# A two-block transformer kernel in which the second block's norms take each reciprocal root as one GpSimd power, and TensorE adds more of the row sums

## The chip, the cores and the metric

The kernel runs on one core of a Trainium2 chip. Its time is the device time of one execution in microseconds; lower is better. All data are 32-bit floats; matrix products are made from values that are split into a high and a low part, three products for each.

## The reference, cut to what matters

256 tokens of 1024 features pass through a first block (an mLSTM mixer and a diff-attention mixer, each with a mixture of experts) and a second block of two layers. Only the norms of the second block matter here. A sub-layer of it computes an output y for one or two streams (stream 0 is x, stream 1 the context ctx; both have 256 tokens), adds it after a norm and a gate, and norms the new stream for the next sub-layer:

```
r1 = rsqrt(mean(y*y) + EPS)               # per token, over D = 1024 features
x  = x + gate * y * r1
r2 = rsqrt(mean(x*x) + EPS)
u  = x * r2 * gain * (1 + scale) + shift  # input of the next sub-layer
```

There are six sub-layers: FFN, mixer (attention), FFN, then FFN, mixer, and a last FFN. The first four have both streams, the last two stream 0 alone.

## The kernel before, in words

The first block ends at about 914 us of the span. The second keeps the streams transposed, features on partitions: x and ctx are 8 tiles of 128 features x 256 tokens (`KT = 8`). Weights come from HBM, are split into `hi` (ScalarE, L371) and `lo` (VectorE, L374) and held in TensorE while the activations `u` or `act` stream through, in threes (L381, L382, L383; below "products").

The class `Output` (L478 to L551) forms the norms of a sub-layer's output. For every output tile d (0 to 7) and stream, `add` (L489) makes one tile `t` of three 128x256 parts, named `ysq` in the trace: y squared (ScalarE, L497), gate*y squared (ScalarE, L498) and gate*y*x (VectorE, L499). d = 0 goes straight to the accumulator `acc`, d = 1 to 5 are added to it by GpSimd and d = 6 by VectorE (L501). For d = 7, `end` lets TensorE sum over features: products of `acc` and of `t` with a matrix of ones, three each (L519), into the PSUM tile `st`. `go_on` delays `end` by one output tile.

`rows(s)` (L532) follows: VectorE copies the sums out of PSUM (`rowsums`, L537), TensorE transposes them (L540, two), VectorE copies 128x6 numbers (`sums`, L541), and `rstd` (L406 to L423) gives r1 in eleven small VectorE instructions on 128x2 (L412 to L422: mean and EPS, a first guess by the bit pattern, two Newton steps). `row` spreads r1 over all partitions by two TensorE transposes (L427, called rb1 here). The sum of squares of the new x is not taken anew: L546 to L549 work it out on 128x2 from the old one, z2 = sum of (gate*y)^2 and xz = sum of gate*y*x. A second `rstd` and a second `row` (rb2) give r2. `update` (L553) then does the stream tile by tile: gate*y*rb1 (L561, VectorE), its addition to x (L562; the first tile VectorE, the others GpSimd), x*gain*rb2 (L569), and the split into `u` (L358, L359 and L361, L362: even tiles by ScalarE and VectorE, odd ones by ScalarE and GpSimd).

The last FFN (`ffn_last`, L728) works by tokens: for each half of 128 tokens it has the sum of squares from ScalarE (L783), the product with the gate (L784), `rstd`, and the final multiply and add (L789) ahead of the store. `start` (L1056) makes the first norm of each stream.

The order on each engine is set when the program is built, by a scheduler that goes by dependences and estimated times; each engine runs its list in order. PSUM has five tiles for products (`mm`), two for transposes (`tp`, where rb1 and rb2 lie too) and one for sums (`st`). Two buffers hold `ysq`.

Names used below: the boundary between two sub-layers with both streams occurs four times, that with stream 0 alone once (into the last FFN, near 2487 us); the boundary after the fourth sub-layer hands over one of the four. "First boundary" is the one near 1277 us.

Of the kernel before, what the change touches and what calls it, by code (L numbers as in the profile page):

```python
# [10 lines left out]
F32 = mybir.dt.float32  # L11
F32R = mybir.dt.float32r
I32 = mybir.dt.int32
AF = mybir.ActivationFunctionType
# [17 lines left out]
READY = 2  # L32

# [201 lines left out]
class Kernel:  # L235
# [188 lines left out]

    def bcast(self, out, col):

        self.nc.tensor.transpose(out, col.to_broadcast([128, 128]), self.ident)  # L427
# [50 lines left out]
    class Output:  # L478
# [10 lines left out]
        def add(self, d, s):  # L489
# [10 lines left out]
            if 0 < d < KT - 1:  # L500
                (nc.vector if d == KT - 2 else nc.gpsimd).tensor_add(self.acc[s], self.acc[s], t)  # L501
# [8 lines left out]
        def end(self, d, s, t):  # L510
            if d == KT - 1:
                self.sums(s, self.acc[s])
                self.sums(s, t)
                self.done(self, s)
# [17 lines left out]
        def rows(self, s):  # L532

            kern, nc, pool = self.kern, self.kern.nc, self.pool
            v = pool.tile([128, 3, 2], F32, tag="sums", name="sums", bufs=2)
            t = pool.tile([128, S], F32, tag="xs", name="rowsums", bufs=kern.xs_bufs)[:96]
            nc.vector.tensor_copy(t, self.st[:96, s * S:s * S + S])  # L537
# [3 lines left out]
            nc.vector.tensor_copy(v, tp.rearrange("p (j q c) -> p q j c", j=2, q=3)[:, :, :, 0])  # L541
            y2, z2, xz = (v[:, q] for q in range(3))
            x2 = pool.tile([128, 2], F32, tag=f"x2_{s}", name="x2", bufs=2)
            r1 = kern.rstd(pool, y2, 2, D, "n")
            rb1 = kern.row(r1)
            nc.vector.tensor_mul(z2, z2, r1)  # L546
            nc.vector.scalar_tensor_tensor(z2, xz, 2.0, z2, op0=ALU.mult, op1=ALU.add)
            nc.vector.tensor_mul(z2, z2, r1)
            nc.vector.tensor_add(x2, self.x2[s], z2)  # L549
            self.x2[s] = x2  # L550
            return rb1, kern.row(kern.rstd(pool, x2, 2, D, "n2"))  # L551
# [176 lines left out]
    def ffn_last(self, ring, pool, u, gate, home, out):  # L728
# [46 lines left out]
        for j in range(2):  # L775
            for f in (NF - 2, NF - 1):
                down(f, j)
            sums = pool.tile([128, 3, 2], F32, tag="sums", name="sums", bufs=2)[:, 0]
# [7 lines left out]
            r = self.rstd(pool, sums, 2, D, "n")[:, :1]  # L786
# [213 lines left out]
    def second_block(self, pool, result):  # L1000
# [3 lines left out]
        for tag, n, b in (*PLACES, ("wraw", 1024, 5)):  # L1004
            pool.tile([128, n], F32R if tag == "act" else F32, tag=tag, name=tag, bufs=b)
        ready, mark = {}, None
# [26 lines left out]

        with self.tc.issue_after(mark.ins):
            self.start(pool, self.u_first, 0)
# [20 lines left out]
    def start(self, pool, u, s):  # L1056

        x2 = self.x2[s] = self.cp.tile([128, 2], F32, name=f"x2_{s}")
        self.nc.vector.tensor_copy(x2, self.x_squares(pool, s))
# [3 lines left out]
        self.pre(pool, u, s, self.row(self.rstd(pool, x2, 2, D, "n")), gs[:, :, 0], mod[:, 0:8, 0])  # L1063
# [801 lines left out]
```

## Time and profile before

| what | value |
|---|---|
| median of 3 runs | 2703.2 us (2702.36 to 2704.69) |
| the profiled execution's own time | 2702.24 us |
| its span in the profile | 2700.4 us |
| TensorE (PE) busy, weight loads (PEld) | 2476.7 us (92%), 1915.4 us (71%) |
| VectorE (DVE) | 1653.1 us (61%) |
| ScalarE (ACT) | 935.7 us (35%) |
| GpSimd (POOL) | 473.4 us (18%) |

Busy times are shares of one execution's span. A timeline row gives start, duration, engine, line, operation, out<-in, count, and in brackets the idle time of that engine just before it with what ended it. The view of waits sums such idle time by instruction and releaser. Line numbers are those of the kernel before; PE, DVE, ACT, POOL and SP are TensorE, VectorE, ScalarE, GpSimd and SyncE.

### The profile page before, as it was taken

How to read it: one execution, taken by the hardware profiler on the slowest of the kernel's cores; microseconds unless marked ns; L12 is line 12 of the kernel's file. 1: busy time of each engine (PE TensorE's matmuls, PEld its weight loads, DVE VectorE, ACT ScalarE, POOL GpSimd, SP SyncE). 2: the span in 40 equal slices, each digit the busy share in tenths (PEclk: the TensorE clock that was granted, in tenths of full speed). 3: DMA queues.
4: the chain of work that ended last, by engine and by line, in shares of the span. 5: the costliest groups of instructions: out<-in, count | busy, mean ns of one | idle time of the engine just before them, and what ended most of it. 6: DMA issues, size and time to landing. Idle time of an engine off the chain costs nothing.

```text
span 2700.4 us, 38571 instructions
## 1 busy us (share of the span) xinstructions
PE 2476.7 (92%) x14614; PEld 1915.4 (71%) x14614; DVE 1653.1 (61%) x3421; ACT 935.7 (35%) x1641; POOL 473.4 (18%) x420
## 2 busy tenths in 40 slices
PE   3988997887999899999899999999899999898998
PEld 3874344566444688888775788888788888786997
DVE  7873125786222368656866777673858665958555
ACT  3541103564011232223327542222432223445543
POOL 2330101544000000002406420000400001534100
PEclk9989998888999899999899999999999999999999
DMA  8789997667999356532340236453247443322453
GB/s 320 276 327 410 420 419 261 232 211 298 381 398 419 141 185 221 168 120 88 135 138 1 79 110 209 154 190 91 74 148 226 155 150 97 118 83 94 160 178 123
DMA packets 123305, 540.62 MB, mean 200 GB/s; under 512 B 14688, under 2 KB 14944, under 8 KB 98272
## 3 DMA queue, kind: packets, MB, share of 16 engines
q1 hardware_dynamic: 123104, 538.00, 55.2%
q8 instruction: 119, 1.95, 0.3%
q14 instruction: 82, 0.67, 0.1%
HBM read 536.90 MB, written 1.05 MB: 199 GB/s over the span
## 4 chain that ended last, share of the span: by engine, by line
PE 56%; DVE 7%; issue 1%; ACT 1%; DMA 1%; POOL 0%; DVEq 0%; SPq 0%; ACTq 0%; POOLq 0%
PE mm L382 16%; PE mm L383 16%; PE mm L381 16%; DVE lo L374 2%; PE tp L383 1%; PE tp L382 1%; PE tp L381 1%; PE mm L868 1%; PE tp L860 1%; PE mm L848 1%; DVE ysq L499 1%; DMA raw<-in_w_ada_dram 1%; ACT hi L371 0%; DVE mx L818 0%; DVE rs_x L412 0%
## 5 line engine op out<-in xcount | busy, mean ns | idle before, releaser
L374 DVE TENSOR_TENSOR lo<-raw,hi 128x512 fp32r<-128x512 f32 (+1 forms) x780 | 574.7, 766 | 381.5 <-ACT hi L371 379.1
L371 ACT ACTIVATE hi<-raw 128x1024 fp32r<-128x1024 f32 (+1 forms) x390 | 404.7, 1044 | 872.3 <-PE mm L382 571.4
L381 PE MATMUL mm<-u,hi 128*128 128x512 f32 (+1 forms) x1608 | 572.8, 360 | 17.5 <-ACT hi L371 9.6
L383 PE MATMUL mm<-u,lo 128*128 128x512 f32 (+1 forms) x1608 | 576.8, 360 | 5.2 <-DVE lo L374 5.2
L382 PE MATMUL mm<-u,hi 128*128 128x512 f32 (+1 forms) x1608 | 578.2, 360 | 2.3 <-POOL u L359 1.3
L381 PEld LDWEIGHTS mm<-u,hi 128*128 128x128 f32 x1608 | 306.9, 193 | 64.5 <-ACT hi L371 11.2
L383 PEld LDWEIGHTS mm<-u,lo 128*128 128x128 f32 x1608 | 310.5, 193 | 49.1 <-DVE lo L374 6.9
L382 PEld LDWEIGHTS mm<-u,hi 128*128 128x128 f32 x1608 | 310.6, 193 | 47.3 <-DVE u L362 2.5
L382 PE MATMUL mm<-act,hi 128*128 128x512 f32 (+1 forms) x612 | 223.0, 364 | 0.1
L381 PE MATMUL mm<-act,hi 128*128 128x512 f32 (+1 forms) x612 | 222.3, 363 | 0.0
L383 PE MATMUL mm<-act,lo 128*128 128x512 f32 (+1 forms) x612 | 222.2, 363 | 0.0
L1691 PE MATMUL mm<-raw,xg 128*32 128x512 f32 x1696 | 199.2, 593 | 1.1 <-DMA raw<-in_moe_gu_dram 1.1
L623 DVE SCALAR_TENSOR_TENSOR junk<-raw,conds 128x1024 f32<-128x1024 f32 x128 | 155.6, 1222 | 66.3 <-DMA raw<-in_w_ada_dram 65.9
L620 POOL TENSOR_TENSOR raw<-raw,cond 128x1024 f32<-128x1024 f32 x48 | 119.9, 2502 | 244.7 <-DMA raw<-in_w_ada_dram 224.8
L501 POOL TENSOR_TENSOR acc<-acc,ysq 128x768 f32<-128x768 f32 x45 | 92.5, 2065 | 394.0 <-DVE ysq L499 348.8
L623 DVE SCALAR_TENSOR_TENSOR raw<-raw,conds 128x1024 f32<-128x1024 f32 x128 | 156.6, 1229 | 2.4
L628 POOL TENSOR_TENSOR mod<-mod,vecs 128x16 f32<-128x16 f32 (+1 forms) x28 | 10.3, 366 | 764.7 <-DVE raw L623 721.4
L1691 PEld LDWEIGHTS mm<-raw,xg 128*32 128x32 f32 x1696 | 63.0, 110 | 112.3 <-issue 107.6
L381 PEld LDWEIGHTS mm<-act,hi 128*128 128x128 f32 x612 | 117.5, 192 | 18.7 <-issue 1.2
L382 PEld LDWEIGHTS mm<-act,hi 128*128 128x128 f32 x612 | 117.7, 192 | 18.2 <-DVE act L351 0.7
L383 PEld LDWEIGHTS mm<-act,lo 128*128 128x128 f32 x612 | 117.5, 192 | 17.2
L1723 DVE TENSOR_TENSOR hy<-hy,tp 128x512 f32<-128x512 f32 x56 | 38.2, 686 | 149.3 <-PE tp L1720 149.1
(458 smaller groups left out, 4102.5 us busy)
## 6 DMA issues: line engine op xcount, KB each, us to landing
raw<-in_moe_gu_dram SPq DMA_DIRECT2D x122, 1024.0 KB, 17.8
raw<-in_w_ada_dram SPq DMA_DIRECT2D x200, 512.0 KB, 4.5
raw<-in_ffn_wi_dram SPq DMA_DIRECT2D x176, 512.0 KB, 4.3
raw<-in_moe_down_dram SPq DMA_DIRECT2D x63, 1024.0 KB, 17.8
raw<-in_ffn_wo_dram SPq DMA_DIRECT2D x48, 448.0 KB, 3.9
raw<-in_w_k_dram SPq DMA_DIRECT2D x32, 512.0 KB, 3.9
raw<-in_ffn_wo_dram SPq DMA_DIRECT2D x24, 512.0 KB, 4.2
raw<-in_ffn_wo_last_dram SPq DMA_DIRECT2D x22, 512.0 KB, 4.1
```

The costliest lines, as they stand in the source:

```text
L371: self.mark = self.nc.scalar.activation(hi[:, :m], raw[:, c:c + m], AF.Copy)
L374: self.nc.vector.tensor_sub(lo[:, i:e], raw[:, c + i:c + e], hi[:, i:e])
L381: nc.tensor.matmul(out, lh, rh, start=start, stop=False, skip_group_check=mixed)
L382: nc.tensor.matmul(out, lh, rl, start=False, stop=False, skip_group_check=mixed)
L383: nc.tensor.matmul(out, ll, rh, start=False, stop=stop, skip_group_check=mixed)
L499: nc.vector.scalar_tensor_tensor(t[:, 2], y, self.gate(d, s), kern.xs(d, s), op0=ALU.mult, op1=ALU.mult)
L501: (nc.vector if d == KT - 2 else nc.gpsimd).tensor_add(self.acc[s], self.acc[s], t)
L620: nc.gpsimd.tensor_mul(out, rows, c)
L623: nc.vector.scalar_tensor_tensor(out, rows, 1.0, c, op0=ALU.mult, op1=ALU.mult, accum_out=mod[:, t, s:s + 1])
L848: nc.tensor.matmul(sc[:, :nk], qk[a][half, 512 + t * 128:640 + t * 128], qk[b][half, :nk], start=(i == 0), stop=(i == 2))
L1691: nc.tensor.matmul(ps[t:t + 32], x[:, t:t + 32], w[i][:, s], start=first, stop=last)
L1723: nc.vector.tensor_add(yv, yv, tp)
```

## The change

- Each `rstd` of `rows`, of `ffn_last` and of the start of stream 0 becomes `rstd2`: one GpSimd instruction that raises a 128x2 tile to the power -0.5 (exponents from a tile `minus_half`). There are 21: two in each of nine `rows`, two in `ffn_last`, one in `start`. The start of stream 1 keeps the VectorE series.
- The sum of squares carried along becomes mean plus EPS, and the new one is put together around r1: the part in z2 uses the reciprocal of m1 (VectorE) instead of r1 squared, so that only the part in xz waits for the power. The numbers are read from PSUM; the copy L541 is gone.
- The copy of the row sums (L537) goes from VectorE to ScalarE.
- `OWN_SUMS = 6, 4`: GpSimd adds d = 1 to 5 (stream 0) or d = 1 to 3 (stream 1); VectorE adds none. The later tiles are summed by TensorE itself, three products of ones for each, each one output tile after its squares. That is one group of three more for stream 0 (five times) and three more for stream 1 (four times): 51 instructions.

```diff
+OWN_SUMS = 6, 4
...
+    def rstd2(self, x, tag):
+
+        y = self.small.tile([128, 2], F32, tag=tag, name="rp_y", bufs=2)
+        self.nc.gpsimd.tensor_tensor(y, x, self.minus_half, op=ALU.pow)
+        return y
...
-            if 0 < d < KT - 1:
-                (nc.vector if d == KT - 2 else nc.gpsimd).tensor_add(self.acc[s], self.acc[s], t)
+            if 0 < d < OWN_SUMS[s]:
+                nc.gpsimd.tensor_add(self.acc[s], self.acc[s], t)
...
         def end(self, d, s, t):
+            if d == OWN_SUMS[s]:
+                self.sums(s, self.acc[s])
+            if d >= OWN_SUMS[s]:
+                self.sums(s, t)
             if d == KT - 1:
-                self.sums(s, self.acc[s])
-                self.sums(s, t)
                 self.done(self, s)
...
-            v = pool.tile([128, 3, 2], F32, tag="sums", name="sums", bufs=2)
             t = pool.tile([128, S], F32, tag="xs", name="rowsums", bufs=kern.xs_bufs)[:96]
-            nc.vector.tensor_copy(t, self.st[:96, s * S:s * S + S])
+            nc.scalar.activation(t, self.st[:96, s * S:s * S + S], AF.Copy)
...
-            nc.vector.tensor_copy(v, tp.rearrange("p (j q c) -> p q j c", j=2, q=3)[:, :, :, 0])
-            y2, z2, xz = (v[:, q] for q in range(3))
-            x2 = pool.tile([128, 2], F32, tag=f"x2_{s}", name="x2", bufs=2)
-            r1 = kern.rstd(pool, y2, 2, D, "n")
+            y2, z2, xz = (tp.rearrange("p (j q c) -> p q j c", j=2, q=3)[:, q, :, 0] for q in range(3))
+            v = kern.small.tile([128, 4, 2], F32, tag="sums", name="sums", bufs=2)
+            m1, inv, w, z = (v[:, i] for i in range(4))
+            nc.vector.tensor_scalar(m1, y2, 1.0 / D, EPS, op0=ALU.mult, op1=ALU.add)
+            r1 = kern.rstd2(m1, "r1")
             rb1 = kern.row(r1)
-            nc.vector.tensor_mul(z2, z2, r1)
-            nc.vector.scalar_tensor_tensor(z2, xz, 2.0, z2, op0=ALU.mult, op1=ALU.add)
-            nc.vector.tensor_mul(z2, z2, r1)
-            nc.vector.tensor_add(x2, self.x2[s], z2)
-            self.x2[s] = x2
-            return rb1, kern.row(kern.rstd(pool, x2, 2, D, "n2"))
+            nc.vector.reciprocal(inv, m1)
+            nc.vector.scalar_tensor_tensor(w, z2, 1.0 / D, inv, op0=ALU.mult, op1=ALU.mult)
+            nc.vector.tensor_add(w, w, self.x2[s])
+            nc.vector.scalar_tensor_tensor(z, xz, 2.0 / D, r1, op0=ALU.mult, op1=ALU.mult)
+            m2 = kern.small.tile([128, 2], F32, tag=f"x2_{s}", name="x2", bufs=2)
+            nc.vector.tensor_add(m2, w, z)
+            self.x2[s] = m2
+            return rb1, kern.row(kern.rstd2(m2, "r2"))
...
-            r = self.rstd(pool, sums, 2, D, "n")[:, :1]
+            nc.vector.tensor_scalar(sums, sums, 1.0 / D, EPS, op0=ALU.mult, op1=ALU.add)
+            r = self.rstd2(sums, "r1")[:, :1]
```

The scheduler puts the instructions in another order with it. In the order of the changed program the lines are higher by 2 to 13: L383 to L385 are the products, L430 the power, L435 `row`, L507 the VectorE square part, L509 the addition to `acc`, L529 the sums, L549 the transposes, L553 to L561 the small steps of `rows`, L573 and L574 the update (L561 and L562 before), L376 `lo`, L727 an addition of the FFN's output.

First place: VectorE at the first boundary, stream 0's `rows`. Before:

```order
L541 COPY sums<-tp 128x6
L412 TENSOR_SCALAR rs_x<-sums 128x2
L413 TENSOR_SCALAR rs_y<-rs_x 128x2
L414 TENSOR_SCALAR rs_z<-rs_x 128x2
L417 TENSOR_SCALAR rs_h<-rs_x 128x2
L415 TENSOR_TENSOR rs_t<-rs_y 128x2
L416 TENSOR_TENSOR rs_t<-rs_t,rs_z 128x2
L418 SCALAR_TENSOR_TENSOR rs_t<-rs_t 128x2
L419 SCALAR_TENSOR_TENSOR rs_y<-rs_t,rs_y 128x2
L715 TENSOR_TENSOR yT<-yT,mm 128x256
L420 TENSOR_TENSOR rs_t<-rs_y 128x2
L499 SCALAR_TENSOR_TENSOR ysq<-yT,gate,ctxT 128x256
```

With the change, on the same engine:

```order
L553 TENSOR_SCALAR sums<-tp 128x2
L376 TENSOR_TENSOR lo<-raw,hi 128x512
L556 RECIPROCAL sums<-sums 128x2
L573 SCALAR_TENSOR_TENSOR xs<-yT,gate,tp 128x256
L557 SCALAR_TENSOR_TENSOR sums<-tp,sums 128x2
L559 SCALAR_TENSOR_TENSOR sums<-tp,rp_y 128x2
L558 TENSOR_TENSOR sums<-sums,x_0_18444 128x2
L574 TENSOR_TENSOR xT<-xT,xs 128x256
L561 TENSOR_TENSOR x_21176<-sums 128x2
L573 SCALAR_TENSOR_TENSOR xs<-yT,gate,tp 128x256
L727 TENSOR_TENSOR yT<-yT,mm 128x256
```

The series and the stream-1 squares between its steps are gone from here; the first update product (L573), which needs rb1, now stands ahead of the steps that lead to the second power, and the squares of stream 1's tiles stand behind stream 0's update.

Second place: TensorE at the same boundary, from the transposes of stream 0's sums to rb2. With the change (before, 26 to 27 products stand between L540, rb1 and the next sums):

```order
L549 MATMUL tp<-consts,rowsums 128x96 x2
L384 MATMUL mm<-act,hi 128x256
L385 MATMUL mm<-act,lo 128x256
L383 MATMUL mm<-act,hi 128x256
L384 MATMUL mm<-act,hi 128x256
L435 MATMUL tp<-consts,rp_y 128x128 x2
...
L529 MATMUL st<-acc,consts 32x256
L435 MATMUL tp<-consts,rp_y 128x128 x2
L529 MATMUL st<-acc,consts 32x256 x2
L529 MATMUL st<-ysq,consts 32x256 x3
```

Four products now stand between the transposes and rb1, and ten and one sum (the rows left out are products) between rb1 and rb2; rb2 stands ahead of stream 1's sums instead of behind them. Behind rb2 follow 42 products and stream 1's sums as far as they are made, and then the 96 products of stream 0's new `u`, with stream 1's last sums, its transposes, rb1 and rb2 among them.

Third place: GpSimd, from the additions of the first boundary on. Before:

```order
L628 TENSOR_TENSOR mod_0_63<-mod_0_63,vecs 128x16 x4
L501 TENSOR_TENSOR acc<-acc,ysq 128x768 x10
L562 TENSOR_TENSOR xT<-xT,xs 128x256 x3
L359 TENSOR_TENSOR u<-xs,u 128x256
L562 TENSOR_TENSOR xT<-xT,xs 128x256 x2
```

With the change:

```order
L640 TENSOR_TENSOR mod_0_63<-mod_0_63,vecs 128x16 x4
L509 TENSOR_TENSOR acc<-acc,ysq 128x768 x8
L430 TENSOR_TENSOR rp_y<-sums,minus_half 128x2
L430 TENSOR_TENSOR rp_y<-x_21176,minus_half 128x2
L574 TENSOR_TENSOR xT<-xT,xs 128x256 x3
L361 TENSOR_TENSOR u<-xs,u 128x256
```

All eight remaining additions of both streams stand ahead of stream 0's first power, and its second power ahead of its update's additions.

## Rows read from the trace of the kernel before

**Rows 1.** The page's busy times and shares of the span.

```profile
PE 2476.7 (92%) x14614; PEld 1915.4 (71%) x14614; DVE 1653.1 (61%) x3421; ACT 935.7 (35%) x1641; POOL 473.4 (18%) x420
```

**Rows 2.** Waits of PE, 1263 to 2700 us: sum, times, longest (us).

```profile
PE tp L427 <- DVE rs_y L422: 22.6, 14, 3.5
PE st L519 <- DVE acc L501: 13.2, 8, 4.3
PE mm L381 <- ACT u L361: 7.8, 7, 1.1
```

**Rows 3.** Timeline of PE, first boundary.

```profile
1276.29 0.28 PE L382 MATMUL mm<-act,hi 128*128 128x256 f32 x1
1276.41 0.28 PE L383 MATMUL mm<-act,lo 128*128 128x256 f32 x1
1277.20 0.63 PE L519 MATMUL st<-acc,consts 128*32 128x256 f32 x6 [0.51 <-DVE acc L501]
...
1286.96 0.66 PE L427 MATMUL tp<-consts,rs_y 128*128 128x128 f32 x2 [2.98 <-DVE rs_y L422]
...
1293.32 0.63 PE L519 MATMUL st<-acc,consts 128*32 128x256 f32 x6 [1.45 <-DVE acc L501]
...
1295.29 0.40 PE L427 MATMUL tp<-consts,rs_y 128*128 128x128 f32 x2 [0.89 <-DVE rs_y L422]
1296.81 1.16 PE L381 MATMUL mm<-u,hi 128*128 128x256 f32 x4 [1.11 <-ACT u L361]
...
1314.41 0.66 PE L427 MATMUL tp<-consts,rs_y 128*128 128x128 f32 x2 [1.93 <-DVE rs_y L422]
1316.19 1.22 PE L381 MATMUL mm<-u,hi 128*128 128x256 f32 x4 [1.11 <-ACT u L361]
```

**Rows 4.** Timeline of DVE, first boundary.

```profile
1274.10 1.87 DVE L499 SCALAR_TENSOR_TENSOR ysq<-yT,gate,xT 128x256 f32<-128x256 f32 x1
...
1285.06 1.76 DVE L422 SCALAR_TENSOR_TENSOR rs_y<-rs_t,rs_y 128x2 f32<-128x2 f32 x1
...
1287.66 0.48 DVE L561 SCALAR_TENSOR_TENSOR xs<-yT,gate,tp 128x256 f32<-128x256 f32 x1 [0.17 <-PE tp L427]
...
1288.59 0.42 DVE L562 TENSOR_TENSOR xT<-xT,xs 128x256 f32<-128x256 f32 x1
...
1307.43 0.16 DVE L412 TENSOR_SCALAR rs_x<-sums 128x2 f32<-128x2 f32 x1
...
1309.01 0.16 DVE L422 SCALAR_TENSOR_TENSOR rs_y<-rs_t,rs_y 128x2 f32<-128x2 f32 x1
```

**Rows 5.** Timeline of POOL, first boundary: the addition of d = 5, stream 0.

```profile
1273.83 1.84 POOL L501 TENSOR_TENSOR acc<-acc,ysq 128x768 f32<-128x768 f32 x1 [0.45 <-DVE ysq L499]
```

**Rows 6.** Window: PE, PEld, DVE, ACT, POOL busy (count); granted clock; DMA share; GB/s.

```profile
1284.00:1290.00 6.00, 3.04 (x15) 3.07 (x16) 5.83 (x16) 1.87 (x3) 2.73 (x2) 0.72 0.19 51
```

**Rows 7.** Groups of POOL instructions by form, whole span: busy, mean ns, idle before.

```profile
L839 POOL TENSOR_TENSOR lo<-proj,hi 128x512 fp32r<-128x512 f32 x12 | 15.5, 1290 | 79.3 <-ACT hi L838 79.3
...
L628 POOL TENSOR_TENSOR mod<-mod,vecs 128x8 f32<-128x8 f32 x12 | 3.8, 318 | 71.5 <-DVE raw L623 28.1 <-ACT raw L621 24.7 <-DMA raw<-in_w_ada_dram 10.4
```

**Rows 8.** Timeline of PE, boundary into the last FFN (stream 0 alone).

```profile
2487.00 1.07 PE L519 MATMUL st<-acc,consts 128*32 128x256 f32 x6 [4.26 <-DVE acc L501]
...
2489.86 0.58 PE L540 MATMUL tp<-consts,rowsums 96*128 96x96 f32 x2 [0.55 <-DVE rowsums L537]
2492.48 0.69 PE L427 MATMUL tp<-consts,rs_y 128*128 128x128 f32 x2 [2.04 <-DVE rs_y L422]
2496.68 0.66 PE L427 MATMUL tp<-consts,rs_y 128*128 128x128 f32 x2 [3.51 <-DVE rs_y L422]
2498.45 0.80 PE L381 MATMUL mm<-u,hi 128*128 128x256 f32 x2 [1.11 <-ACT u L361]
```

**Rows 9.** Timeline of DVE, the end of the last FFN.

```profile
2690.27 0.17 DVE L412 TENSOR_SCALAR rs_x<-sums 128x2 f32<-128x2 f32 x1
...
2695.93 1.41 DVE L789 SCALAR_TENSOR_TENSOR yg<-yg,rs_y,rows 128x512 f32<-128x512 f32 x2
```

More of the change, by code (lines that the diff above doesn't have):

```diff
@@ L777, in ffn_last @@
                 down(f, j)
-            sums = pool.tile([128, 3, 2], F32, tag="sums", name="sums", bufs=2)[:, 0]
+            sums = self.small.tile([128, 4, 2], F32, tag="sums", name="sums", bufs=2)[:, 0]
             t = pool.tile([128, D], F32, tag="pt", name="yg", bufs=2)
@@ L1005, in second_block @@
             pool.tile([128, n], F32R if tag == "act" else F32, tag=tag, name=tag, bufs=b)
+        self.small = pool
         ready, mark = {}, None
@@ L1032, in enter @@
             self.update(pool, u[s], s, out, gs[:, :, s], mod[:, i * 8:(i + 1) * 8, s])
+        self.minus_half = pool.tile([128, 2], F32, name="minus_half")
+        nc.gpsimd.memset(self.minus_half, -0.5)
         with self.tc.issue_after(mark.ins):
@@ L1058, in start @@
         x2 = self.x2[s] = self.cp.tile([128, 2], F32, name=f"x2_{s}")
-        self.nc.vector.tensor_copy(x2, self.x_squares(pool, s))
+        st = self.x_squares(pool, s)
+        self.nc.vector.tensor_scalar(x2, st, 1.0 / D, EPS, op0=ALU.mult, op1=ALU.add)
         mod = self.mod2[0][:, :, s:s + 1]
@@ L1062, in start @@
         u = u[..., s * S:s * S + S]
-        self.pre(pool, u, s, self.row(self.rstd(pool, x2, 2, D, "n")), gs[:, :, 0], mod[:, 0:8, 0])
+        self.pre(pool, u, s, self.row(self.rstd(pool, st, 2, D, "n") if s else self.rstd2(x2, "r1")), gs[:, :, 0], mod[:, 0:8, 0])
     def x_rows(self, pool):
```

## The prediction, made before the changed kernel had run

> **What bounds the kernel now.** The page comes first: TensorE is busy 92% of the span and no other engine over 61% [rows 1]. So time is gained where TensorE stands still, or nowhere. The view of TensorE's waits, cut to the second block, names three that the change touches [rows 2]: 22.6 us for `rs_y` (the eleven-step series ahead of a broadcast), 13.2 us for `acc` (the last addition ahead of the sums), 7.8 us for the first `u`. Together 43.6 us, 1.6% of the span; the change cannot gain much more. The timeline of the first boundary shows them in turn [rows 3]: 0.51 for `acc`, 2.98 for `rs_y`, then 1.45, 0.89 and 1.11, and for stream 1 1.93 and 1.11: 9.98 us. The boundary into the last FFN [rows 8] has 4.26 + 2.04 + 3.51 + 1.11 = 10.9 us. The other three boundaries share the remaining 43.6 - 10.0 - 10.9 = 22.7 us.
>
> Two more things are to be seen. The series needs 1.74 us where VectorE has nothing else (from its first step at 1307.43 to the end of its last at 1309.17), and much longer where larger work stands between its steps: its last step at 1285.06 alone took 1.76 us [rows 4]. And after the wait of 2.98 us the granted clock is 0.72 in the window of 6 us around it [rows 6]: part of it ran at 1.2 instead of 2.4 GHz. Of the 15 instructions there that kept TensorE busy 3.04 us, 13 are products; at the spacing of 0.12 us that rows 3 show at 1276 they need 1.6 us, the two transposes 0.3. Some 1.2 us are lost to the clock, and they don't show as a wait.
>
> **The price of a power, p.** Nothing in the trace shows this operation. The least is what a small GpSimd instruction takes: 0.318 us for 128x8 [rows 7]; so p is not below 0.3. The most that I allow is each of the eleven steps at that price: 3.5 us; I take 3.3 with the smaller tile. GpSimd's two rows give 1290 - 318 = 972 ns for 504 more elements per partition, 1.9 ns each, and a fixed 0.30. I take **p = 0.75 us**: the fixed part, and for two elements as much as 230 of an addition's. It is nearer to the low end because it is one instruction of the kind of the 128x8 row, and not eleven that wait for one another.
>
> **First boundary.** The last product of d = 7 ends its issue at 1276.5 [rows 3]; with stream 0's sums of `acc` and d = 6 taken one tile earlier in the order, 21 products (2.5 us) stand behind them. They are reached at 1274.0, but must wait for the VectorE part of d = 6, until 1275.97 [rows 4]; GpSimd's addition of d = 5 is done at 1275.67 [rows 5]. The wait moves forward; it doesn't go. But VectorE's addition of d = 6 and with it the squares of d = 7 behind it are gone from the chain. Sums to 1276.5, 21 products to 1279.0, three sums to 1279.5 (their row is 0.63 long with its drain [rows 3]), seven products, the transposes, four products to 1281.1. Mean, hop, power, hop: rb1 at 1281.2 + p, against 1286.96. To rb2 I count 1.85 us and one more power: a product of 0.48, an addition of 0.42 [rows 4], and four small steps with their hops of about 0.2 each: rb2 at 1283.5 + 2p, against 1295.29. Behind it TensorE has 42 products and nine sums (some 6.5 us); the first of `u` came 1.5 us after rb2 before (1295.29 to 1296.81) [rows 3], so it is hidden: 1290.0 + 2p against 1296.81, a gain of 6.8 - 2p.
>
> Stream 1 then: 96 products (11.5 us), its remaining sums (1.0), the transposes (0.3), the attention's small sums that stand there anyway (0.8), 1.4 for squares that VectorE now does behind stream 0's update, and two powers with a net 2p, whose hops (0.3 less, 0.25 more) nearly cancel. The added groups of sums of both streams are in these figures. First product of stream 1's `u` at 1306.2 + 4p, against 1316.19: **gain 9.9 - 4p**. The reciprocal and the sums of the new x run beside the power and cost nothing; if the power were short they would be the end, at most 0.4 us. ScalarE's copy of the row sums is taken as no longer than VectorE's; ScalarE is busy 35% [rows 1].
>
> **The other places.** The three other boundaries: 22.7 - 12p, by the same ratio of gain to wait. Into the last FFN TensorE has nothing between: without VectorE's addition of 768 columns (by the 0.42 us for 256 [rows 4], about 1 us) the transposes come at about 2489.0 instead of 2489.86 [rows 8] (from the d = 5 and d = 6 tiles being ready, the three more sums are free in that wait); then rb1 at 2489.9 + p, rb2 at 2491.4 + 2p against 2496.68: 5.3 - 2p. At the end of `ffn_last` [rows 9], from the first series (2690.27) the half's path is power, two final products (1.41), the second half's two gate products (1.4), power: the last pair starts at 2693.9 + 2p against 2695.93: 2.0 - 2p. In `start` a power takes the place of a series that is hidden now: -p + 0.1. Bias loads and conditioning loads swap places on SP's queue; no transfer is on the path there, so nothing.
>
> Sum: 9.9 + 22.7 + 5.3 + 2.0 + 0.1 = 40.0, less (4 + 12 + 2 + 2 + 1) p = 21p. At p = 0.75 that is 24.3 us. From it I take 5 us, for a stretch of lower clock at each of four boundaries that may stay (1.2 us each), since the sums at 1276 still follow a wait. Gain 19.3: 2702.24 - 19.3 = **2683 us**, against the profiled execution's own time; that one is 1.0 us under the median of the runs, which is too little to change anything.
>
> A rule of the Trainium skill bears on the power ("SBUF — State Buffer", on who interferes with whom): a GpSimd instruction that reads SBUF holds a port pair shared with VectorE to its end, and VectorE's instructions with two SBUF inputs wait. The rows agree: L499 took 1.87 us and L422 1.76 beside GpSimd's additions of 1.84 [rows 4, 5], the latter 0.16 elsewhere. By the rule the subtractions of the weight split could be held up behind each power; 8 times some 0.4 us would make the gain 3 us smaller. The sum does without it.
>
> **Rivals.**
> (a) *The power is dear.* GpSimd stands in the chain between transposes and rb1, and between rb1 and rb2, with nothing of the next tile to do meanwhile. With 21 of them the sum is zero at p = 40/21 = 1.9, or at 35/21 = 1.67 with the clock's 5 us taken off; slower by 0.2% of 2703, 5.4 us, from p = 1.9. At 2.5 it gives 2702.2 - 35 + 52.5 = 2720 us, at 3.3 2736. For it: the rows show no power, and additions of 128x2 to 128x8 on GpSimd cost 0.318 against VectorE's 0.16 [rows 4, 7]. Against: it takes more than six small GpSimd instructions' time in one. Chance 0.14. The Trainium skill ("GPSIMD Engine Reference", engine selection) calls GpSimd the wrong place for elementwise arithmetic that VectorE can do; the rows agree in the price of one step, and the case here is one step for eleven.
> (b) *The wait moves.* VectorE still has the weight splits, and now does the squares of stream 1's last tiles after stream 0's update; TensorE's sums of d = 4 to 7 wait for them in order, with stream 0's products queued behind. If each boundary gives back half, the gain is 24.3/2 = 12 with the clock as before, less if the wait is where the clock falls: 2690 to 2697. For it: VectorE is busy 5.83 of 6 us in the window [rows 6]. Against: it has less to do by 9 x 22 small steps and nine additions. Chance 0.15.
> (c) *Nothing comes of it*: p between 1.4 and 1.9, or (b) to the full; within 0.2%, 2698 to 2708. Chance 0.12.
> (d) *All of it and more*: p near 0.3, no stretch at the lower clock: 40.0 - 21 x 0.33 = 33 us: 2669. Chance 0.1.
>
> **How the numbers follow.** The forecast itself has 0.49. Faster by over 0.2% (about what a measurement of this kernel can tell from no change): 0.49 + 0.15 + 0.1 = 0.74; same 0.12; slower 0.14. The range leaves out a little beneath (d), 2667, and the dear power above p = 1.9: up to 2707.
>
> **What would show it.** Right: the row of the power near 0.75 us; the waits for `rs_y` gone, those for the power at most 1.5 us each, and the waits for the sums not above their 13.2; rb2 of the first boundary about 10 us earlier and stream 1's `u` about 7; the wait of 3.51 into the last FFN near 1.5. Wrong: a power of over 1.7 us, or waits of the sums for L507's squares that exceed what the series took.

## The result

| | before | changed |
|---|---|---|
| median | 2703.94 us (2702.36 to 2707.82, 4 runs) | 2675.26 us (2667.9 to 2677.85, 4 runs) |
| ratio to before | 1 | 0.9887, 95% interval 0.9864 to 0.9911 |
| the profiled execution, its span | 2702.24, 2700.4 us | 2673.1, 2671.3 us |

The change makes the kernel 1.1% faster, by 24 to 37 us over the interval of the ratio. A second set of runs, beside others further below, gave 0.9892 (0.9867 to 0.9916). The forecast was 2683 us, within 2667 to 2707.

The waits of TensorE from 1263 us on, to be read against [rows 2] (sum, times, longest):

```profile
PE tp L435 <- POOL rp_y L430: 10.9, 17, 1.4
PE st L529 <- POOL acc L509: 5.4, 4, 1.5
PE mm L861 <- ACT p L835: 4.7, 4, 2.3
PE st L529 <- ACT ysq L505: 1.9, 2, 1.1
...
PE mm L384 <- POOL u L361: 1.6, 2, 1.0
```

The attention's wait (L861 here, L848 before) is the same 4.7 us in both. The wait for the root has halved, 22.6 to 10.9, although it now occurs 17 times; that for the sums went from 13.2 to 7.3 (5.4 and 1.9); that for ScalarE's part of `u` from 7.8 to 1.8, while GpSimd's part is waited for 1.6 us. No wait listed for roots or sums is longer than 1.5 us; before, the longest were 3.5 and 4.3.

The timeline of TensorE in the changed kernel: the second block's first product, the first boundary [rows 3], the one into the last FFN [rows 8], and the last product:

```profile
908.21 0.39 PE L383 MATMUL mm<-u,hi 128*128 128x256 f32 x1 [4.25 <-ACT hi L373]
...
1273.28 0.63 PE L529 MATMUL st<-acc,consts 128*32 128x256 f32 x6 [1.50 <-POOL acc L509]
...
1278.48 0.33 PE L549 MATMUL tp<-consts,rowsums 96*128 96x96 f32 x2
...
1280.22 0.43 PE L435 MATMUL tp<-consts,rp_y 128*128 128x128 f32 x2 [0.92 <-POOL rp_y L430]
...
1282.67 0.43 PE L435 MATMUL tp<-consts,rp_y 128*128 128x128 f32 x2 [0.27 <-POOL rp_y L430]
...
1289.89 0.28 PE L383 MATMUL mm<-u,hi 128*128 128x256 f32 x1
...
1307.25 0.39 PE L384 MATMUL mm<-u,hi 128*128 128x256 f32 x1
...
2463.45 0.58 PE L549 MATMUL tp<-consts,rowsums 96*128 96x96 f32 x2 [0.51 <-ACT rowsums L546]
2465.06 0.69 PE L435 MATMUL tp<-consts,rp_y 128*128 128x128 f32 x2 [1.03 <-POOL rp_y L430]
2467.16 0.69 PE L435 MATMUL tp<-consts,rp_y 128*128 128x128 f32 x2 [1.42 <-POOL rp_y L430]
...
2662.58 0.39 PE L385 MATMUL mm<-hi,act 128*128 128x512 f32 x1
```

And the first and last product of the kernel before:

```profile
910.65 0.39 PE L381 MATMUL mm<-u,hi 128*128 128x256 f32 x1 [3.98 <-ACT hi L371]
...
2690.83 0.39 PE L383 MATMUL mm<-hi,act 128*128 128x512 f32 x1
```

The changed kernel's execution is 2.4 us ahead when the second block begins (908.21 for 910.65), so 2.4 is to be added before a row at the first boundary is set beside one of before. rb1 then comes 4.3 us earlier, rb2 10.2, stream 0's first `u` 4.5; and that has no wait ahead of it. The 97th product of the new `u`, at which stream 1's began before (1316.19), comes at 1307.25, 6.5 us earlier. Into the last FFN the wait of 3.51 [rows 8] is now 1.42.

Where the time went is read most safely from TensorE's own products, since the first block of the kernel, which the change leaves alone, differs by up to 15 us from one profiled execution to the next (the second block's first product stood between 902.1 and 917.3 us in the traces of this study). Before the second block takes 1780.2 us between them, changed 1754.4: 25.8 us less. The same distance is used below ("second block"), with the tail from the last product to the end of the span (9.58 us before, 8.75 changed). By boundary, from one group of products to the next: 7.6, 5.3, 7.1 and 3.7 us at the four with both streams, 2.7 at and behind the one into the last FFN (3.9 as far as `u`, of which 1.2 are lost behind it); between them the two traces differ by up to 0.6.

The clock moved too. TensorE over windows around the five boundaries (busy, count, granted clock, DMA share, GB/s), before and then changed:

```profile
1245.00:1325.00 80.00, 69.82 (x457) 0.91 0.25 79
1500.00:1590.00 90.00, 82.17 (x544) 0.96 0.19 62
1870.00:1970.00 100.00, 90.15 (x557) 0.95 0.21 66
2250.00:2350.00 100.00, 91.50 (x533) 0.95 0.30 93
2440.00:2520.00 80.00, 67.27 (x486) 0.89 0.31 99
```

```profile
1245.00:1325.00 80.00, 75.29 (x533) 1.00 0.29 92
1500.00:1590.00 90.00, 87.82 (x586) 1.00 0.30 103
1870.00:1970.00 100.00, 96.16 (x612) 1.00 0.31 105
2250.00:2350.00 100.00, 94.97 (x611) 0.98 0.37 120
2440.00:2520.00 80.00, 72.89 (x511) 0.91 0.47 147
```

Before, the four boundaries with both streams had eleven stretches at the lower of the two levels (1.2 GHz), 41.0 us together: not only behind the waits of about 3 us but also, at 1296.91 and 1313.97, behind waits of 1.45, 0.89 and 1.11 and at the end of one of 1.93 [rows 3]. In the changed kernel one of 3.4 us is left, at the fourth. Another 3.4 us lie just behind the end of the first window, at 1325.03, and no wait of over 0.3 us stands in the 15 us ahead of it:

```profile
1325.00:1329.00 4.00, 4.00 (x12) 0.57 0.64 223
```

Into the last FFN 13.7 of 17.1 us are left; there TensorE still stands still between sums, roots and `u`. Half of the time at half the clock is lost where TensorE is busy; by that estimate the 37.6 us less at the four boundaries are worth up to 19 us, not much below the 24 us by which the waits fell (together more than the gain, of which the 51 added products of ones, at 0.15 us each, take back 7.7). No run separates the two.

The powers, as the view of their line gives them (min/median/max in ns, first and last start, forms):

```profile
L430 POOL TENSOR_TENSOR rp_y<-sums,minus_half x11: 695/1077/1082, 1279.1 to 2666.1; 128x2 f32<-128x2 f32 x11
L430 POOL TENSOR_TENSOR rp_y<-x,minus_half x10: 690/694/703, 924.4 to 2466.4; 128x2 f32<-128x2 f32 x10
```

One power takes 0.69 us, or 1.08: 0.84 on the mean of 21 (0.75 had been taken).

### The profile page after: what moved, and what is told of

Same layout as the page of the kernel before. It is cut to its first block, busy times and chain, and to the rows that moved or that the text cites. A ratio compares the mean times of both kernels' runs of the same rounds, so it can differ in the third digit from the quotient of the medians.

```text
span 2671.3 us, 38559 instructions
## 1 busy us (share of the span) xinstructions
PE 2478.4 (93%) x14716; PEld 1908.5 (71%) x14716; DVE 1598.7 (60%) x3182; ACT 933.7 (35%) x1651; POOL 474.6 (18%) x434
## 4 chain that ended last, share of the span: by engine, by line
PE 59%; DVE 4%; POOL 2%; issue 1%; ACT 1%; DMA 0%; DVEq 0%; POOLq 0%; SPq 0%; ACTq 0%
PE mm L383 16%; PE mm L384 16%; PE mm L385 16%; PE tp L385 1%; PE tp L384 1%; PE tp L383 1%; PE mm L881 1%; DVE lo L376 1%; PE mm L861 1%; PE tp L873 1%; PE st L529 1%; POOL rp_y L430 1%; PE mm L946 1%; PE mm L947 1%; PE mm L948 1%
## 5 line engine op out<-in xcount | busy, mean ns | idle before, releaser
L376 DVE TENSOR_TENSOR lo<-raw,hi 128x512 fp32r<-128x512 f32 (+1 forms) x780 | 568.3, 758 | 379.0 <-ACT hi L373 377.0
L383 PE MATMUL mm<-u,hi 128*128 128x512 f32 (+1 forms) x1608 | 575.0, 359 | 11.7 <-ACT hi L373 9.9
L385 PE MATMUL mm<-u,lo 128*128 128x512 f32 (+1 forms) x1608 | 573.2, 358 | 4.6 <-DVE lo L376 4.5
L383 PEld LDWEIGHTS mm<-u,hi 128*128 128x128 f32 x1608 | 307.0, 191 | 57.6 <-ACT hi L373 11.5
L385 PEld LDWEIGHTS mm<-u,lo 128*128 128x128 f32 x1608 | 306.9, 191 | 50.4 <-DVE lo L376 7.9
L383 PE MATMUL mm<-act,hi 128*128 128x512 f32 (+1 forms) x612 | 221.4, 362 | 0.0
L385 PE MATMUL mm<-act,lo 128*128 128x512 f32 (+1 forms) x612 | 220.4, 360 | 0.0
L509 POOL TENSOR_TENSOR acc<-acc,ysq 128x768 f32<-128x768 f32 x37 | 74.9, 2037 | 365.1 <-DVE ysq L507 347.3
L383 PEld LDWEIGHTS mm<-act,hi 128*128 128x128 f32 x612 | 115.4, 189 | 22.4 <-issue 4.9
L385 PEld LDWEIGHTS mm<-act,lo 128*128 128x128 f32 x612 | 115.5, 189 | 17.1
```

What stands on the lines that cost most here:

```text
L376: self.nc.vector.tensor_sub(lo[:, i:e], raw[:, c + i:c + e], hi[:, i:e])
L383: nc.tensor.matmul(out, lh, rh, start=start, stop=False, skip_group_check=mixed)
L385: nc.tensor.matmul(out, ll, rh, start=False, stop=stop, skip_group_check=mixed)
L509: nc.gpsimd.tensor_add(self.acc[s], self.acc[s], t)
```

## The experiments

Eleven further kernels ran, and the changed one again, each beside runs of the kernel before on the same chip. Gains in the table are from the ratio (times 2703 us) and, in the last columns, from one profiled execution each. The two traces of the changed kernel differ by 2.8 us in the second block, so a difference of that size decides nothing.

| kernel | ratio (95%) | gain, us | second block, us | tail, us |
|---|---|---|---|---|
| before | 1 | | 1780.2 | 9.6 |
| changed | 0.9887 (0.9864 to 0.9911) | 30.5 | 1754.4 | 8.7 |
| changed, again | 0.9892 (0.9867 to 0.9916) | 29.2 | 1751.6 | 8.7 |
| powers alone | 0.9983 (0.9966 to 1.0001) | 4.6 | 1773.7 | 8.7 |
| algebra alone | 0.9963 (0.9948 to 0.9978) | 10.0 | 1769.3 | 9.6 |
| sums alone | 0.9947 (0.9929 to 0.9966) | 14.3 | 1772.2 | 9.6 |
| powers and algebra | 0.9955 (0.9934 to 0.9977) | 12.2 | 1765.4 | 8.7 |
| all but the powers | 0.9901 (0.9879 to 0.9923) | 26.8 | 1758.5 | 9.6 |
| all but powers and ScalarE copy | 0.9915 (0.9893 to 0.9937) | 23.0 | 1755.5 | 9.6 |
| all but the ScalarE copy | 0.9893 (0.9874 to 0.9913) | 28.9 | 1754.8 | 8.7 |
| powers only with one stream | 0.9916 (0.9898 to 0.9934) | 22.7 | 1758.8 | 8.7 |
| each power twice | 0.9941 (0.9918 to 0.9965) | 15.9 | 1762.7 | 10.3 |
| OWN_SUMS = 5, 4 | 0.9910 (0.9889 to 0.9931) | 24.3 | 1758.4 | 8.7 |
| OWN_SUMS = 6, 6 | 0.9935 (0.9922 to 0.9949) | 17.6 | 1757.9 | 8.8 |

**Taking the change apart.** First the sums as before, with the powers and the new algebra left in (and VectorE's copy):

```diff
-            if 0 < d < OWN_SUMS[s]:
-                nc.gpsimd.tensor_add(self.acc[s], self.acc[s], t)
+            if 0 < d < KT - 1:
+                (nc.vector if d == KT - 2 else nc.gpsimd).tensor_add(self.acc[s], self.acc[s], t)
...
-            if d == OWN_SUMS[s]:
-                self.sums(s, self.acc[s])
-            if d >= OWN_SUMS[s]:
-                self.sums(s, t)
             if d == KT - 1:
+                self.sums(s, self.acc[s])
+                self.sums(s, t)
```

> The changed kernel with the sums as before (GpSimd adds d = 1 to 5, VectorE d = 6, TensorE only the accumulator and d = 7) and VectorE's copy of the row sums; the powers and the new algebra stay. Theory A (most of the gain is the series taken out of the chain): TensorE's waits ahead of the broadcasts fall from 22.6 to about 11 us and those for the accumulator stay near 13; 14 to 18 us of the changed kernel's 28.7 us remain: 2686 to 2690 us. Theory B (the gain is the sums that TensorE takes and the order they bring; the powers only replace one wait by another): at most 6 us remain, 2697 us or more.

12.2 us remain (2690.8 us median): between the two theories. The waits for the root are 15.4 us in 18 times, those for the accumulator 7.6, and that for GpSimd's half of `u` (L361) has grown from 1.3 us in three times to 11.3 in 12.

The opposite, the kernel before with the sums alone (the same lines the other way round):

> The kernel before with only the sums changed (GpSimd adds d = 1 to 5 or d = 1 to 3, TensorE takes the later tiles); series and copies as before. Theory A: the waits for the accumulator fall from 13.2 to about 5 us and VectorE has nine additions of 0.95 us less, the series' waits stay or grow: a gain of 5 to 10 us, 2694 to 2699 us. Theory B: 15 us or more, 2689 us or less.

14.3 us by the times (2690.3 us), near theory B's 15, though the wait for the accumulator falls from 13.2 to 5.3, as theory A had it; the runs of this kernel lie between 2679.6 and 2702.5 us. The second block of the profiled execution is only 8.0 us shorter. But the boundaries there gain 15.5; 7.6 are lost again in the second sub-layer's products, far from any norm, in a stretch at the lower clock that none of the other 13 traces has at that place:

```profile
1478.00:1499.00 21.00, 20.73 (x81) 0.51 0.15 50
```

TensorE's waits in the 15 us ahead of it are 0.51 us and less. With one trace of this kernel it stays open whether it is always there. The two parts together make 26.5 of some 30 us by the times, so there they hardly overlap; what the first part owes to the power was open.

The series put back behind the changed mean step, everything else as changed:

```diff
     def rstd2(self, x, tag):
-        y = self.small.tile([128, 2], F32, tag=tag, name="rp_y", bufs=2)
-        self.nc.gpsimd.tensor_tensor(y, x, self.minus_half, op=ALU.pow)
-        return y
+        x2, h, y, t = (self.small.tile([128, 2], F32, tag=tag + c, name="rs_" + c, bufs=2) for c in "zhyt")
...
+        nc.vector.scalar_tensor_tensor(y, t, 1.5, y, op0=ALU.add, op1=ALU.mult)
+        return y
```

> The changed kernel with each power taken back to the ten further VectorE steps of the series, behind the same mean step; the algebra, ScalarE's copy and TensorE's sums stay. Theory A: the series' length (1.74 us alone, more between larger work) stands in the chain again in place of 0.69 to 1.08 us: 12 to 20 us slower than the changed kernel, 2687 to 2695 us. Theory B: within 6 us of it.

This is the study's main run. 26.8 us of gain are left without a single power there (2678.64 us): theory A falls. In the second block it is 4.1 and 6.9 us behind the two traces of the changed kernel. TensorE's waits:

```profile
PE tp L446 <- DVE rs_y L441: 6.7, 4, 3.1
PE mm L383 <- ACT u L363: 6.6, 7, 1.1
PE st L540 <- POOL acc L520: 5.3, 4, 1.5
```

TensorE waits for the series at four transposes, 6.7 us, less than the 10.9 that it waits for the powers (it waits more for `u`). Of the 6.7, 5.0 are into the last FFN, where stream 0 is alone:

```profile
2469.96 0.43 PE L446 MATMUL tp<-consts,rs_y 128*128 128x128 f32 x2 [1.83 <-DVE rs_y L441]
...
2473.54 0.66 PE L446 MATMUL tp<-consts,rs_y 128*128 128x128 f32 x2 [3.15 <-DVE rs_y L441]
```

At the first boundary its timeline shows how the longer chain is covered:

```profile
1279.93 0.33 PE L560 MATMUL tp<-consts,rowsums 96*128 96x96 f32 x2
...
1283.22 0.38 PE L446 MATMUL tp<-consts,rs_y 128*128 128x128 f32 x2
...
1288.90 0.40 PE L446 MATMUL tp<-consts,rs_y 128*128 128x128 f32 x2
```

From the transposes of the sums to rb1 are 3.3 us and to rb2 9.0, against 1.7 and 4.2 in the changed kernel. But there are 16 products and six sums ahead of rb1 here and 38 products with three sums behind it, and neither broadcast has a wait. The order that the scheduler makes for a longer chain puts more of stream 1's products into it. In the changed kernel four products stand ahead of rb1, and it waits 0.92. At this boundary the series even comes out ahead (table further below); at the next two it is 1.7 to 1.9 us behind.

Then the algebra alone and the power alone, each in the kernel before:

> The kernel before with the algebra alone: mean plus EPS carried, the numbers read from PSUM without the copy, the z2 part made from a reciprocal beside the series, so that two small steps instead of five lie between the two series. Series, VectorE's copy and the sums as before. Theory F (the algebra is the largest single part, since it shortens a VectorE chain whose steps stand between larger work): 10 us or more faster than the kernel before, 2693 us or less, and about what power and algebra together give (2691 us). Theory A (the power is what makes that pair work): at most 5 us faster, 2698 us or more.

The edit is the part of the diff in `rows` from `y2, z2, xz` on, with the ten steps of the series in `rstd2`. 10.0 us (5.9 to 14.1), 10.9 in the second block: theory F, just, since the median (2695.24 us) misses its 2693; theory A's 5 us lie outside the interval. 8.5 of the 10.9 come from the first boundary.

> The kernel before with the 21 powers alone: the copy of the sums, the old algebra (r1 squared, four steps behind the first power) and the sums as before. Theory A: 10 us or more faster, 2693 us or less. Theory F: at most 6 us faster, since each boundary keeps the copy and the four steps behind the first root.

```diff
-            r1 = kern.rstd(pool, y2, 2, D, "n")
+            r1 = kern.rstd2(y2, "r1")
...
-            return rb1, kern.row(kern.rstd(pool, x2, 2, D, "n2"))
+            return rb1, kern.row(kern.rstd2(x2, "r2"))
```

(`rstd2` is here a mean step on VectorE and the power.) 4.6 us, with an interval that touches zero; 6.5 in the second block and 0.9 at the end. The waits say why so little: 20.2 us for the power in 15 times, and 10.1 for GpSimd's half of `u`.

```profile
PE tp L435 <- POOL rp_y L430: 20.2, 15, 2.7
PE mm L382 <- POOL u L359: 10.1, 14, 1.7
```

With the copy and the four old steps around it, the power only replaces the wait for `rs_y` by one for `rp_y`. By boundary (the same products as above; the fifth is into the last FFN with what is behind it), in us gained on the kernel before:

| kernel | first | second | third | fourth | fifth |
|---|---|---|---|---|---|
| changed | 7.6 | 5.3 | 7.1 | 3.7 | 2.7 |
| changed, again | 7.6 | 5.3 | 7.1 | 4.7 | 4.1 |
| powers alone | 4.0 | 1.4 | 2.1 | -2.2 | 2.1 |
| algebra alone | 8.5 | 1.4 | 2.8 | -1.1 | -0.3 |
| sums alone | 7.0 | 2.3 | 2.5 | 2.9 | 0.8 |
| all but the powers | 9.6 | 3.5 | 5.4 | 2.2 | 1.4 |
| all but powers and ScalarE copy | 10.2 | 3.9 | 4.4 | 3.7 | 1.5 |
| powers only with one stream | 10.0 | 4.0 | 4.2 | 1.6 | 3.8 |

The parts do not simply add. At the first boundary each alone takes most of what the whole takes, at the fourth only the sums take anything alone. That 6.5, 10.9 and 8.0 us in the second block come near the whole's 25.8 and 28.6 is chance, since the 8.0 hold the loss of 7.6 from above.

**The price of a power.** Each power twice into the same tile:

```diff
         self.nc.gpsimd.tensor_tensor(y, x, self.minus_half, op=ALU.pow)
+        self.nc.gpsimd.tensor_tensor(y, x, self.minus_half, op=ALU.pow)
```

> The changed kernel with each of its 21 powers taken twice into the same tile, so that the second doubles the time on GpSimd and its result is the same. The forecast's slope, 21 p with every power in the chain: 21 x 0.69 = 14.5 us slower than the changed kernel, near 2690 us, the waits for the powers up from 11.4 to about 24 us. If TensorE's products behind each power hide it: within 4 us of 2675.

13 to 15 us slower than the changed kernel by the ratios (0.9941 against 0.9892 and 0.9887), 8.3 in the second block (11.1 against its second trace) and 1.5 in the tail; the waits for the powers nearly double:

```profile
PE tp L436 <- POOL rp_y L431: 20.2, 18, 2.2
```

By the times the forecast's slope holds and a power's time is all in the chain; by the traces two thirds to nine tenths of it are.

**The copy.** The row sums copied by VectorE again:

```diff
-            nc.scalar.activation(t, self.st[:96, s * S:s * S + S], AF.Copy)
+            nc.vector.tensor_copy(t, self.st[:96, s * S:s * S + S])
```

> The changed kernel with the row sums copied by VectorE again. Theory C (the copy matters because VectorE has other work in hand when the sums are done): the transposes come later by the rest of a VectorE instruction at each of nine places, 0.3 to 0.7 us each: 3 to 6 us slower than the changed kernel. Theory D (a copy is a copy): within 1.5 us of it in the trace, and no difference that the times can tell.

1754.8 against 1754.4 and 1751.6 us, and 0.9893 against 0.9887 and 0.9892: theory D, as closely as two traces of one kernel agree. The same with the series:

> The changed kernel with the series in place of the powers and the row sums copied by VectorE; what is left of the change is TensorE's sums and the algebra (mean carried, numbers read from PSUM, the z2 part made beside the root). It splits the 13.7 us that lie between the sums alone and the kernel with all but the powers. Theory C: the copy has 5 us or more of them. Theory D: the algebra and the order that it brings have them nearly all, and this kernel is within 2 us of the one with ScalarE's copy and the series.

0.9915 against 0.9901 by the times, with intervals that overlap, and 3 us less in the second block, of which 1.4 fall before the first boundary, where no sums are copied. Theory C has nothing for it; D's 2 us were missed on the other side.

**Where the power belongs.** The series at the four boundaries with both streams, the power elsewhere (the new third argument of `rstd2` picks the series):

```diff
-            r1 = kern.rstd2(m1, "r1")
+            r1 = kern.rstd2(m1, "r1", len(self.streams) > 1)
...
-            return rb1, kern.row(kern.rstd2(m2, "r2"))
+            return rb1, kern.row(kern.rstd2(m2, "r2", len(self.streams) > 1))
```

> The changed kernel with the series at the boundaries with both streams and the power only where stream 0 is alone (into the last FFN, its end, the start). Theory E (with two streams TensorE's products cover the series once VectorE is relieved, and the power is worth something only where nothing covers it): equal to the changed kernel within 3 us, and 1.5 to 3 us faster than the kernel with the series everywhere. Theory A (the power is worth about as much at each place): 3 us slower than the changed kernel, near the kernel with the series everywhere.

Neither fully. From the last attention's products to those of the last FFN this kernel gains 3.8 us on the kernel before and the one with the series everywhere 1.4, so the power is worth 2.4 us there, where nothing covers a chain, as theory E says; against the two traces of the changed kernel (2.7 and 4.1) it is 1.3 and 2.7. The end agrees: the tail is 9.6 us in each kernel with the series there and 8.7 to 8.8 in each with a single power. But by the whole this kernel is not faster than the series everywhere (0.9916 against 0.9901): the same series came out 1.6 us worse in this trace between the first boundary and the last attention. Nor is it equal to the changed kernel: at the second and third boundary all three kernels with the series there gain 1.3 to 2.9 us less than either trace of the changed one, at the fourth up to 3.1 less, and at the first 2.0 to 2.7 more. So the power is worth something with two streams too.

**How many sums.** TensorE takes one tile of stream 0 more:

```diff
-OWN_SUMS = 6, 4
+OWN_SUMS = 5, 4
```

> The changed kernel with OWN_SUMS = 5, 4: TensorE takes d = 5 of stream 0 too, in five places. In the changed kernel TensorE waits 1.50 us for GpSimd's addition of d = 5 at four of them. If that wait is the end there, it falls to the wait for the squares of d = 6: at most 1.0 us gained for each less 0.45 for three more products of ones, 2 to 3 us in all. If VectorE's squares end last anyway: 2 us slower (five times 0.45).

4 us longer in the second block (6.8 against the second trace), by the times not to be told from the changed kernel. The wait that was to go was of some 1.5 us at three boundaries, not four (the fourth of the 5.4 us in four times is 0.81, into the last FFN). It does not go: TensorE now comes to the sums one output tile earlier and waits there for GpSimd's addition of d = 4, and the products of ones are paid.

```profile
PE st L529 <- POOL acc L509: 5.2, 3, 1.7
```

Then two of stream 1 less:

```diff
-OWN_SUMS = 6, 4
+OWN_SUMS = 6, 6
```

> The changed kernel with OWN_SUMS = 6, 6: GpSimd adds d = 4 and 5 of stream 1 too, at four boundaries, and TensorE takes 24 products of ones less. Theory G (GpSimd is now in the chain): two additions of some 2 us each stand on GpSimd's list near stream 0's powers and updates; TensorE's wait for the accumulator or the powers grows by 1 to 2 us at each of the four: 4 to 8 us slower than the changed kernel. Theory H (GpSimd has time, TensorE has not): 24 x 0.15 = 3.6 us less on TensorE, so up to 3.6 us faster.

Theory G, and more: 0.9935 against 0.9892, 12 us slower. In the second block it is 3.5 us, or 6.3 against the second trace; the rest lies in the first block, which the edit leaves alone, so some of the 12 is scatter. The lists of GpSimd and VectorE at the first boundary show a part of the mechanism:

```profile
1286.39 1.08 POOL L430 TENSOR_TENSOR rp_y<-sums,minus_half 128x2 f32<-128x2 f32 x1 [5.87 <-DVE sums L553]
1287.44 1.83 POOL L509 TENSOR_TENSOR acc<-acc,ysq 128x768 f32<-128x768 f32 x1
1289.78 0.70 POOL L430 TENSOR_TENSOR rp_y<-x,minus_half 128x2 f32<-128x2 f32 x1 [0.51 <-DVE x L561]
```

```profile
1288.58 0.71 DVE L558 TENSOR_TENSOR sums<-sums,x 128x2 f32<-128x2 f32 x1
```

An addition of stream 1 of 1.83 us now stands between stream 0's two powers. It is over 0.5 us before the second power starts, so it does not keep GpSimd from it; but VectorE's step L558 beside it takes 0.71 us, to the end of the addition, where it never takes over 0.17 in the changed kernel, and rb2 waits 0.91 us for 0.27. And TensorE's waits for the accumulator double, from 5.4 us in four times to 10.6 in eight; the four new ones, of 1.06 to 1.91 us, stand ahead of stream 1's sums:

```profile
PE st L529 <- POOL acc L509: 10.6, 8, 1.9
```

> The changed kernel once more, beside the two parts on the same chip, for an interval and to see how far its trace differs from one execution to another: 26 to 31 us faster than the kernel before, and each boundary within 1 us of the first trace.

29.2 us by the ratio. The first three boundaries agree within 0.3 us, the fourth and the one into the last FFN were 1.0 and 1.5 better, so the expected 1 us was missed at the last. No kernel of the study beats the changed one.

## Why the prediction was right, and where it was not

*Bound and places.* Right: TensorE's three waits fell from 43.6 us to some 20 (10.9, 7.3 and 1.8), and each boundary gave some of it. At the first boundary the 97th product of the new `u` came 6.5 us earlier and the products behind it 7.6 (6.9 forecast), into the last FFN 3.9 as far as `u` (3.8 forecast) and 2.7 behind it, at the end 0.8 (0.5 forecast), the other three 16.0 together (13.7 forecast). In `start`, where 0.65 us were to be lost, nothing moved. Two steps of the working do not add up as written. From rb1 to rb2 it counts 1.85 us besides the power, but its two times lie 2.3 apart; measured were 2.45 with a power of 0.69, so 1.76. And the terms named for stream 1 make 15.0 us, where its times lie 16.2 apart; for the 1.2 us between them no row is given. With the named terms alone the gain at the first boundary would have been some 8.5 us, further from what was measured.

*The price of a power.* 0.84 us on the mean for 0.75; the slope of 21 p was 13 to 15 us by the times, 9.8 in the trace (12.6 against the second one), for 14.5 when each was doubled. The dear power, the rival on the slower side, did not occur.

*The 5 us for the clock.* This is the term of the sum that failed. The deduction assumed that the stretches at the lower level stay at four boundaries, because the sums still follow a wait. They don't: the granted clock is 1.00, 1.00, 1.00 and 0.98 around these, for 0.91 to 0.96 before, and 3.4 of 41.0 us at the lower level are left, with another 3.4 just behind the first window. Nor was there one stretch at each boundary before, but two or three. Nor did the length of a wait alone decide: in the kernel with the algebra alone one of 2.73 us, until 1293.0, was followed by none. Without the deduction the sum was 24.3 us, against 25.8 in the second block and 0.8 in the tail; with the measured 0.84 us for a power it was 40.0 - 21 x 0.84 = 22.4, so the places gave some 4 us more than their terms. The remaining difference to the 29 of the times is no larger than what executions of one kernel differ by.

*What carries the gain.* The forecast gave it to the power: it treated a chain with a long root as one that pays 21 times its length, with nothing left at p = 1.9. For a power on GpSimd the slope held; for the series that it replaces it did not. Put back, with 1.6 us and more for each root, it should have left 40 - 21 x 1.6 = 6 us; 26.8 were left by the times, 21.7 in the second block. So the time came out right, but not for the reason that the form of the sum gives. The order is remade for each chain, and with two streams it has products to put there. What counted was the work around the root: two small steps between the roots in place of four and a mean, and no copy ahead of the first (10.9 us alone), and fewer additions on VectorE and GpSimd, with TensorE's sums in their place (14.3 us alone by the times, 15.5 at the boundaries of its trace). That the power's share cannot be fixed more closely than 1 to 7 us, by which kernel it is read from, is left open. So is the share of the order itself: no kernel ran with the order held fixed.

The forecast saw one more thing in the series' way, in L422 [rows 4], and did not price it. The small VectorE steps of the norms take 0.16 us, but in the kernel before 18 of the 256 from the first boundary on are longer, by 17.2 us together, and each of the 18 ends within 0.03 us of the end of a GpSimd instruction that had started ahead of it. At the first boundary L412 in the series for r1 is another:

```profile
1281.00 1.62 DVE L412 TENSOR_SCALAR rs_x<-sums 128x2 f32<-128x2 f32 x1
```

```profile
1280.03 2.58 POOL L501 TENSOR_TENSOR acc<-acc,ysq 128x768 f32<-128x768 f32 x1 [4.35 <-DVE lo L374]
1284.99 1.81 POOL L501 TENSOR_TENSOR acc<-acc,ysq 128x768 f32<-128x768 f32 x1 [2.39 <-ACT ysq L498]
```

L412 and L422 lose 3.1 us beside GpSimd's additions, about as much as the 2.98 us that TensorE then waits for rb1. In the changed kernel no VectorE step of the norms is held up so; with the sums alone it is 5.5 us, with the series put back 5.0, with the algebra alone still 16.0. So a part of what looks like the price of a long series is the price of where GpSimd's additions stand, and that the change moves too. How much of the 17.2 us was in the chain, no run shows.

*Port.* The sentence on the shared port pair had the size right and the side wrong. VectorE's subtraction goes first and the power waits:

```profile
1278.85 0.16 DVE L553 TENSOR_SCALAR sums<-tp 128x2 f32<-128x2 f32 x1
1278.92 0.68 DVE L376 TENSOR_TENSOR lo<-raw,hi 128x512 fp32r<-128x512 f32 x1
...
1300.00 0.68 DVE L376 TENSOR_TENSOR lo<-raw,hi 128x512 fp32r<-128x512 f32 x1
```

```profile
1279.08 1.08 POOL L430 TENSOR_TENSOR rp_y<-sums,minus_half 128x2 f32<-128x2 f32 x1 [5.86 <-DVE sums L553]
...
1281.92 0.69 POOL L430 TENSOR_TENSOR rp_y<-x,minus_half 128x2 f32<-128x2 f32 x1 [1.76 <-DVE x L561]
...
1299.77 0.70 POOL L430 TENSOR_TENSOR rp_y<-x,minus_half 128x2 f32<-128x2 f32 x1 [1.75 <-DVE x L561]
```

The subtraction starts at 1278.92, takes its usual 0.68 us and ends at 1279.60; the power that starts at 1279.08 ends at 1280.16, some 0.56 after it. The eight powers of 1.08 us are those of r1 at the boundaries with both streams, where the order puts a subtraction behind the mean step. The other thirteen took 0.69 to 0.70. 8 x 0.38 = 3.0 us. The Trainium skill ("SBUF — State Buffer", who interferes with whom) says that the issue order decides which of the two is held; where the subtraction goes first, the trace agrees, with the power as the one held. Where the power goes first, it shows no hold: at four second powers a subtraction starts 0.23 us behind the power (1300.00 behind 1299.77) and takes its usual 0.68 us. So the 3 us that the forecast feared for VectorE did not come up.

*The other rivals.* The wait did move, to the first sums (1.5 us at three boundaries and 0.81 into the last FFN for GpSimd's last addition), but with the 1.9 us for squares it is about half of the 13.2 that were there. The transfers on SP's queue that swap places ended in no wait of TensorE that wasn't there before.

## What to carry to other kernels

A chain of small steps that several engines pass along is priced by what stands between its steps and by what the order finds to put beside it, not by the length of its longest part; put the old part back into the new order before giving it the credit. Where nothing else is to be done, the length of the part counts: with one stream alone TensorE waits 1.83 and 3.15 us for two series and 1.03 and 1.42 for two powers. Small steps of a chain can also be long because of another engine: look for those that end with one of its instructions. And the stretches at the lower clock went when the waits became shorter, so they belong into the sum; but the length of one wait did not tell whether a stretch followed it, and no run here separates the two.

## What had not been expected of the hardware

A GpSimd power of two elements per partition takes 0.69 us, some 0.37 more than an addition of eight (0.318) [rows 7], so by that estimate its work per element is dear beside 1.9 ns for an addition, but small beside eleven VectorE steps of 0.16 with their hops. A subtraction of VectorE that starts 0.16 us ahead of it makes it 1.08. A VectorE step of 0.16 us that starts behind a GpSimd addition of 1.8 to 2.6 us can last to the end of that addition, up to 1.8 us. And TensorE's clock, which fell behind waits of 3 us at four boundaries and behind shorter ones too, was 1.00 around the first three of them where no wait was longer than 1.5 us.
